# Weight pre-sums, product order and pair order in a one-core encoder layer

## The chip, the core and the metric

The kernel runs on one core of a Trainium2 chip. Its engines work in parallel, each through an instruction queue of its own, in order: TensorE (PE, matmul, with its weight loads shown as PEld), VectorE (DVE), ScalarE (ACT), GpSimd (POOL) and SyncE (SP), which issues most DMAs. The metric is device time of one execution in microseconds (us); lower is better.

## The reference

One layer of a streaming encoder over 1024 prompt rows and 32 sample rows of width 1024, in float32. Cut to what matters here:

```
h = rms_norm(x, g_mix)
q, k, v, ch, cb, cc, ga, gb = split(h @ w_in)          # one input projection, 6656 columns
a  = window_attention(q, k, v) @ w_attn_out
u  = cc * ch
bo = (cb * causal_conv3(u)) @ w_conv_out
x  = x + (sigmoid(ga) * a + sigmoid(gb) * bo) @ w_mix_out
x  = x + cross_attention(rms_norm(x) @ w_cq, mem_k, mem_v) @ w_co
x  = x + square(relu(rms_norm(x) @ w_up)) @ w_down     # 1024 -> 4096 -> 1024
y  = rms_norm(x, g_final)
```

The outputs also hold the last K/V rows, the convolution state and the memory K/V.

## The kernel before

**Layout.** Activations are kept transposed, features on the 128 partitions and rows along the free axis, in three chunks of rows: chunk 0 and 1 of 384, chunk 2 of 288 (`CH`, L23). Every float32 operand is split in a rounded high part and the rest (`split`, L119: a cast on ACT at L120, a subtraction on DVE at L121), and a product is three matmuls: high by high, high by low, low by high (`gemm`, L171 to L178). Weights come in tiles of 128x1024 on SP's queue (`fetch_w`), two ahead, and are split likewise.

**Stages.** (1) Start: load x, scale it by the norm's gain (L256, L257), sums of squares (`squares`, L301), first keys and values. (2) Attention: blocks of scores, softmax and values, interleaved with input projections. POOL scales the softmax rows there (L550). (3) The pairs. (4) The last gate columns and the attention output (`do_attn_out`, L982). (5) Conv-out, mix, cross-attention and the first up columns, chunk beside chunk. `do_conv_out` (L1036) multiplies its product by a gate (DVE, L1045), adds the attention part on POOL (L1048) and splits the sum for the mix product. (6) Pairs of up columns. (7) The down product.

**Pairs.** In stages 3 and 6 two weight tiles times chunks 0 and 1 are computed by a Strassen-like scheme with seven half-size products in place of eight. It needs combinations of activations (`x_kind`, L765, tiles tk and X) and of weights (`pair_issue`, L801: four additions on POOL, L807 to L810, give tiles s for the weights numbered 3 and 4; every one of the four weights is then split). `XP` (L835) lists the 13 pairs of stage 3: C, H and B of columns 4 to 7 (the convolution), then b (one gate) of 2 to 7, then a (the other gate) of 0 to 7. `x_pair` (L881) computes one pair and calls `after(name)` at named points (B11, W1, W4, W3, W2), where the next pair's loads and weights are issued. The first product of a pair (`x_p1`, L863) is copied by ACT to a tile s1 (L867) before the second (`x_p2`, L870) is accumulated on the same PSUM tile. Chunk 2 gets plain products (`x_c2`, L874, PSUM tile pa). `x_start` (L933) does these for the first two pairs ahead of the loop. A C column ends in a DVE and a POOL multiply (L596, L597), an H column in a DVE multiply (L601), a B column in three taps and two multiplies, a gate column in a DVE multiply and a sigmoid on ACT (L643, L644) with a store to sg_d.

**Weight sums.** The down product's scheme needs sums of four quarters of each of 32 pieces of `w_down`. `sum_step` (L705) issues from POOL a load of the next piece into SBUF (L710), then makes the four additions for the piece loaded one call earlier (L715) and issues from POOL its store to wsum_d (L716). Tiles alternate between `xacc` (one buffer, free during the whole first half) and `ws` (one buffer in the current stage's pool, L701 to L703). Calls are written at three slots of each of the four attention rounds (L730), and 22 times in stage 4 (L1001 to L1011).

**Order of the work.** The program text gives a priority, not the final order: a planner with a simulated timeline lays out each engine's queue ahead of time, may put a ready instruction ahead of one written before it, and the queues then run in that fixed order.

Of the kernel before, what the change touches and what calls it, by code (L numbers as in the profile page):

```python
# [18 lines left out]
P = 128  # L19
# [19 lines left out]
def hybrid_step(ctx: ExitStack, tc: tile.TileContext, io):  # L39
# [5 lines left out]
    def nm(s):  # L45
        uid[0] += 1
        return f"{s}_{uid[0]}"
# [221 lines left out]
    def norm_x():  # L269
# [31 lines left out]
        def squares(c):  # L301

            n = CH[c][1]
            sums = []
            for e, h in ((dve, 0), (pool_e, 4)):
                acc = st.tile([P, n], F32, tag=f"sum{h}", bufs=2 - h // 4, name=nm("sum"))
                for f in range(h, h + 4):
                    sq = acc if f == h else tmp(n)
                    if c == 0 and h:
                        pool_e.tensor_tensor(sq, raws[c][:, f], raws[c][:, f], op=ALU.mult)  # L310
                    else:
                        act.activation(sq, raws[c][:, f], AF.Square)
                    if f > h:
                        e.tensor_tensor(acc, acc, sq, op=ALU.add)
                sums.append(acc)
            accs[c] = sums
# [379 lines left out]
    W = {}  # L696
    pieces = [(j, t, i) for j in range(4) for t in range(2) for i in range(4)]

    def sum_tile(n):

        if n % 2:  # L701
            return xacc_tile()[:, :1024].rearrange("p (q c) -> p q c", q=4)
        return W["pool"].tile([P, 4, 256], F32, tag="ws", name=nm("ws"))  # L703

    def sum_step(load=True):  # L705
        old = W.pop("new", None)
        if load and pieces:
            at = pieces.pop(0)
            t = sum_tile(len(pieces))
            pool_e.dma_start(t, io["w_down"][at])  # L710
            W["new"] = at, t
        if old:
            at, t = old
            for to, x, y in ((3, 2, 3), (2, 0, 2), (0, 0, 3), (1, 1, 0)):
                pool_e.tensor_tensor(t[:, to], t[:, x], t[:, y], op=ALU.add)  # L715
            pool_e.dma_start(wsum_d[at], t)  # L716

    for kv, starts in enumerate([(0, 1, 3, 5, 6, 8, 10, 11, 13)] * 3 + [(0, 1, 3, 4, 6, 7, 8, 10, 11)]):
        base = 15 * kv
        units = [Unit(kv, p) for p in range(9)]  # L720
        for unit, k in zip(units, starts):
            at(base + k + 3, unit.values)
        for unit, k in zip(units, starts):
            at(base + k, unit.scores)
        for unit, k in zip(units, starts):
            at(base + k + 2, unit.turn)
        if kv < 3:
            at(base + 10, lambda kv=kv: do_KS(kv + 1))
            at(base + 14, lambda kv=kv: do_KS_rest(kv + 1))
        for k in (3, 8, 13):  # L730
            at(base + k, sum_step)
    at(59, lambda: sum_step(False))
    for i, h in enumerate(h for stage in hosts for h in stage):
        extras = [(c, e) for c in range(2) for e in events.get(3 * i + c + 1, [])]
        pre = events.get(3 * i, [])
# [96 lines left out]
        issue_w()  # L832


    XP = [((w, f), (w, f + 1)) for f in (4, 6) for w in "CHB"]  # L835
    XP += [(("b", f), ("b", f + 1)) for f in (2, 4, 6)] + [(("a", f), ("a", f + 1)) for f in (0, 2, 4, 6)]
    LATE = 3
    xs1, xemit = {}, {}

# [76 lines left out]
    def x_steps(i):  # L916
# [6 lines left out]
            todo["B11"] = lambda: x_fetch(i + 1)  # L923

        def after(what):
            todo.get(what, lambda: None)()
            if what == "B11" and XP[i][0][0] == "a" and "cv_cm" in S:
                closed(S.pop("cv_cm"))
                G["pool"] = ctx.enter_context(tc.tile_pool(name="gb", bufs=5, reuse_waits="tile", side="right"))
# [2 lines left out]

    def x_start():  # L933
        x_issue(0, 4)
        x_p2(0, x_p1(0))
        x_c2(0, 0)
        x_issue(0, 3)
        x_c2(0, 1)
        x_p2(1, x_p1(1))
        x_c2(1, 0)  # L940

    def s_begin():
# [59 lines left out]
    for f in range(4):  # L1002
        item(do_attn_out(f, range(3), [(0, sum_step)]), ("w_attn_out", f))
    for f in range(4, NF):
        item(do_attn_out(f, (0,), [(0, sum_step)]), ("w_attn_out", f))
    item(lambda: todo.extend((bcp, bc_d, 0, k) for k in range(NF)))
    for f in range(4, NF):
        item(do_attn_out(f, (2,), [(2, sum_step), (2, lambda: loads(2))]), ("w_attn_out", f))
    item(lambda: todo.extend((bcp, bc_d, 2, k) for k in range(NF)))
    for f in range(4, NF):  # L1010
        item(do_attn_out(f, (1,), [(1, sum_step), (1, lambda: loads(2))]), ("w_attn_out", f))  # L1011
    run()
    while pieces or "new" in W:
        sum_step()
    todo.extend((bcp, bc_d, 1, k) for k in range(NF))
    closed(W["cm"])
    closed(x_cm)
# [230 lines left out]
    def up_part(w, c, j):  # L1248
# [7 lines left out]
        else:  # L1256
            dve.tensor_scalar_max(t, a, 0.0)
        h = tmp(n)
        pool_e.tensor_tensor(h, t, t, op=ALU.mult)  # L1259
        hidden(c, j, h)  # L1260

    def do_up(j, c):
# [250 lines left out]

    def up_start():
        up_issue(0, 4)
        up_p2(0, up_p1(0))
        up_c2(0, 0, 1)
        up_issue(0, 3)
        up_c2(0, 1, 2)
        up_p2(1, up_p1(1))  # L1520
        up_c2(1, 0, 1)

    def up_steps(i):
# [20 lines left out]


    def up_last(i):
        up_p2(i, up_p1(i))
        wanted.extend([op_of("b11", k) for k in range(8)] + [h2_of(0, k) for k in range(8)])
        wanted.extend(op_of("b11", k) for k in range(8, 16))
        pump(4)  # L1550
        up_c2(i, 0, 1)
        pump(4)
        up_c2(i, 1, 2)
        pump(4)
        up_pair(i, up_steps(i), 2)
# [264 lines left out]
```

## Time and profile before

| | us |
|---|---|
| median of 3 runs | 1819.1 |
| the runs | 1818.11, 1819.1, 1920.33 |
| profiled execution | 1824.92 |
| its span, first to last instruction | 1823.0 |
| PE busy in the span | 1749.4 |
| DVE, ACT, POOL busy | 1205.6, 810.7, 755.4 |

Mean granted TensorE clock: 0.985 of full speed. A line of the timeline reads: start, duration, engine, line, operation, output<-inputs, shape, count, and in brackets how long the engine had been idle before it and what ended that. A line of a group reads: line, engine, operation, count | busy us in total, mean ns | idle before. A line of the waits reads: who waited for whom, total us, times, longest. Where the reading of one source line is shown, the durations are minimum/median/maximum in ns, then the first and last start.

### The profile page before, as it was taken

How to read it: one execution, taken by the hardware profiler on the slowest of the kernel's cores; microseconds unless marked ns; L12 is line 12 of the kernel's file. 1: busy time of each engine (PE TensorE's matmuls, PEld its weight loads, DVE VectorE, ACT ScalarE, POOL GpSimd, SP SyncE). 2: the span in 40 equal slices, each digit the busy share in tenths (PEclk: the TensorE clock that was granted, in tenths of full speed). 3: DMA queues.
4: the chain of work that ended last, by engine and by line, in shares of the span. 5: the costliest groups of instructions: out<-in, count | busy, mean ns of one | idle time of the engine just before them, and what ended most of it. 6: DMA issues, size and time to landing. Idle time of an engine off the chain costs nothing.

```text
span 1823.0 us, 30096 instructions
## 1 busy us (share of the span) xinstructions
PE 1749.4 (96%) x11016; PEld 1724.2 (95%) x11016; DVE 1205.6 (66%) x2080; ACT 810.7 (44%) x1561; POOL 755.4 (41%) x789
## 2 busy tenths in 40 slices
PE   6899999999899999997999989999999989999997
PEld 6899999999899999996999989999999989999997
DVE  7778786765867567455666777776656676436674
ACT  7546564554322335233465655642222343334453
POOL 4578868463654233323425152375654400100002
PEclk9999999999999999998999999999999999999998
DMA  6454433214122325688775767663343587446573
GB/s 223 155 186 147 153 129 104 74 55 139 65 70 78 111 85 178 217 282 283 275 244 198 244 209 249 237 211 133 138 138 125 162 291 231 154 133 204 191 252 104
DMA packets 177684, 312.50 MB, mean 171 GB/s; under 512 B 18016, under 2 KB 137600, under 8 KB 177408
## 3 DMA queue, kind: packets, MB, share of 16 engines
q1 hardware_dynamic: 168320, 277.02, 45.5%
q0 software_dynamic: 9216, 33.56, 5.2%
q8 instruction: 87, 1.43, 0.3%
q14 instruction: 61, 0.50, 0.1%
HBM read 232.70 MB, written 77.81 MB: 170 GB/s over the span
## 4 chain that ended last, share of the span: by engine, by line
PE 68%; DMA 15%; DVE 6%; POOL 5%; issue 4%; ACT 2%; SPq 1%; POOLq 0%; DVEq 0%; ACTq 0%
PE acc L176 7%; PE acc L177 7%; PE acc L178 7%; PE acc L825 6%; PE acc L826 6%; PE acc L827 6%; PE acc L1585 5%; PE acc L1586 5%; PE acc L1584 5%; DMA ws<-in_w_down 3%; DMA wsum_d<-ws 2%; POOL ws L715 2%; PE pa L177 2%; PE pa L176 2%; PE pa L178 2%
## 5 line engine op out<-in xcount | busy, mean ns | idle before, releaser
L121 DVE TENSOR_TENSOR wl<-wr,wh 128x1024 fp32r<-128x1024 f32 x222 | 301.5, 1358 | 110.5 <-ACT wh L120 106.4
L120 ACT CAST wh<-wr 128x1024 fp32r<-128x1024 f32 x222 | 233.0, 1049 | 313.1 <-PE acc L177 85.4
L176 PE MATMUL acc<-X,wh 128*128 128x384 f32 (+1 forms) x624 | 206.9, 332 | 12.9 <-ACT wh L120 9.9
L176 PE MATMUL acc<-Y,wh 128*128 128x384 f32 (+1 forms) x624 | 203.2, 326 | 13.0 <-ACT wh L120 12.7
L253 POOL TENSOR_TENSOR xacc<-xacc,ct 128x384 f32<-128x384 f32 (+1 forms) x62 | 77.2, 1247 | 319.2 <-ACT ct L251 317.0
L177 PE MATMUL acc<-X,wh 128*128 128x384 f32 (+1 forms) x624 | 205.0, 329 | 4.3 <-DVE X L257 4.3
L178 PE MATMUL acc<-X,wl 128*128 128x384 f32 (+1 forms) x624 | 204.6, 328 | 0.4 <-DVE wl L121 0.4
L178 PE MATMUL acc<-Y,wl 128*128 128x384 f32 (+1 forms) x624 | 202.4, 325 | 0.3 <-DVE wl L121 0.3
L177 PE MATMUL acc<-Y,wh 128*128 128x384 f32 (+1 forms) x624 | 202.3, 325 | 0.1
L550 POOL TENSOR_SCALAR S<-S,rec 128x256 f32<-128x256 f32 (+1 forms) x132 | 123.9, 951 | 25.6 <-DVE rec L548 25.4
L176 PEld LDWEIGHTS acc<-X,wh 128*128 128x128 f32 x624 | 119.6, 192 | 14.0 <-ACT wh L120 9.9
L176 PEld LDWEIGHTS acc<-Y,wh 128*128 128x128 f32 x624 | 117.7, 189 | 14.8 <-ACT wh L120 13.0
L177 PEld LDWEIGHTS acc<-X,wh 128*128 128x128 f32 x624 | 119.6, 192 | 6.0 <-DVE X L257 4.7
L178 PEld LDWEIGHTS acc<-X,wl 128*128 128x128 f32 x624 | 119.3, 191 | 1.8 <-DVE wl L121 0.9
L178 PEld LDWEIGHTS acc<-Y,wl 128*128 128x128 f32 x624 | 117.8, 189 | 0.8 <-DVE wl L121 0.8
L177 PEld LDWEIGHTS acc<-Y,wh 128*128 128x128 f32 x624 | 117.9, 189 | 0.3 <-DVE Y L121 0.3
L1584 PE MATMUL acc<-Y,wh 128*128 128x384 f32 (+1 forms) x352 | 113.2, 322 | 0.8 <-DVE lt L1362 0.7
L1585 PE MATMUL acc<-Y,wh 128*128 128x384 f32 (+1 forms) x352 | 113.2, 322 | 0.3 <-DVE Y L121 0.2
L1586 PE MATMUL acc<-Y,wl 128*128 128x384 f32 (+1 forms) x352 | 113.0, 321 | 0.0
L120 ACT CAST wh<-s 128x1024 fp32r<-128x1024 f32 x50 | 52.5, 1050 | 102.1 <-PE acc L826 57.3
L807 POOL TENSOR_TENSOR s<-wr 128x512 f32<-128x512 f32 x25 | 36.1, 1445 | 146.9 <-DVE wl L121 130.4
L1259 POOL TENSOR_TENSOR ct<-ct 128x288 f32<-128x288 f32 (+1 forms) x48 | 44.9, 936 | 117.4 <-DVE ct L1255 47.6
(359 smaller groups left out, 5312.7 us busy)
## 6 DMA issues: line engine op xcount, KB each, us to landing
wr<-in_w_in SPq DMA_DIRECT2D x56, 512.0 KB, 3.3
wr<-in_w_up SPq DMA_DIRECT2D x48, 512.0 KB, 3.8
wr<-in_w_down SPq DMA_DIRECT2D x32, 512.0 KB, 3.7
wr<-wsum_d SPq DMA_DIRECT2D x32, 512.0 KB, 3.6
wl<-wl_d SPq DMA_DIRECT2D x28, 512.0 KB, 4.6
wr<-in_w_conv_out SPq DMA_DIRECT2D x24, 512.0 KB, 4.8
wr<-in_w_mix SPq DMA_DIRECT2D x24, 512.0 KB, 4.6
ct<-b_d SPq DMA_DIRECT2D x48, 192.0 KB, 3.9
```

Of the source, the lines that this page charges most:

```text
L120: act.copy(hi, src)
L121: dve.tensor_sub(lo, src, hi.bitcast(F32))
L176: pe.matmul(out, wh[:, a], hi, start=(k == 0), stop=False)
L177: pe.matmul(out, wh[:, a], lo, start=False, stop=False)
L178: pe.matmul(out, wl[:, a], hi, start=False, stop=(k == len(acts) - 1))
L550: pool_e.tensor_scalar_mul(stl[:, h, :nk], stl[:, h, :nk], rec[:, h : h + 1])
L825: pe.matmul(acc, wh[:, a], hi, start=(start and k == 0), stop=False, skip_group_check=True)
L826: pe.matmul(acc, wh[:, a], lo, start=False, stop=False, skip_group_check=True)
L827: pe.matmul(acc, wl[:, a], hi, start=False, stop=(k == 3), skip_group_check=True)
L1584: pe.matmul(a, wh[:, s], hi, start=(start and k == 0), stop=False, skip_group_check=True)
L1585: pe.matmul(a, wh[:, s], lo, start=False, stop=False, skip_group_check=True)
L1586: pe.matmul(a, wl[:, s], hi, start=False, stop=(stop and k == len(acts) - 1), skip_group_check=True)
```

## The change

Five edits.

1. Sums of squares at the start: the four squares of chunk 0 that POOL made go to ACT.
2. Weight sums: two calls in each attention round in place of three (slots 5 and 12), 8 pieces; one piece in each of the 13 pairs, loaded into xacc after W3 and added and stored at the next pair's B11; the other 11 in stage 4, where the calls of the chunk-2 and chunk-1 columns are dropped.
3. Pair order: the gate pairs b(2,3) and b(4,5) come first, the rest follows as before.
4. `x_start`, `up_start` and `up_last`: the chunk-2 product of a pair is written between its first and second product.
5. Up stage: the square of the eight plain chunk-2 up columns goes from POOL to ACT.

```
@@ squares
-                    if c == 0 and h:
-                        pool_e.tensor_tensor(sq, raws[c][:, f], raws[c][:, f], op=ALU.mult)
-                    else:
-                        act.activation(sq, raws[c][:, f], AF.Square)
+                    act.activation(sq, raws[c][:, f], AF.Square)
@@ weight sums
-    def sum_tile(n):
-        if n % 2:
-            return xacc_tile()[:, :1024].rearrange("p (q c) -> p q c", q=4)
-        return W["pool"].tile([P, 4, 256], F32, tag="ws", name=nm("ws"))
-    def sum_step(load=True):
-        old = W.pop("new", None)
-        if load and pieces:
+    def sum_load(acc):
+        W["acc"] = acc
+        if pieces:
             at = pieces.pop(0)
-            t = sum_tile(len(pieces))
+            if acc:
+                t = xacc_tile()[:, :1024].rearrange("p (q c) -> p q c", q=4)
+            else:
+                t = W["pool"].tile([P, 4, 256], F32, tag="ws", name=nm("ws"))
             pool_e.dma_start(t, io["w_down"][at])
             W["new"] = at, t
+    def sum_add(old):
         if old:
             at, t = old
             for to, x, y in ((3, 2, 3), (2, 0, 2), (0, 0, 3), (1, 1, 0)):
                 pool_e.tensor_tensor(t[:, to], t[:, x], t[:, y], op=ALU.add)
             pool_e.dma_start(wsum_d[at], t)
+    def sum_step():
+        old = W.pop("new", None)
+        sum_load(not W.get("acc", True))
+        sum_add(old)
+    def sum_done():
+        sum_add(W.pop("new", None))
-        for k in (3, 8, 13):
+        for k in (5, 12):
             at(base + k, sum_step)
-    at(59, lambda: sum_step(False))
+    at(59, sum_done)
@@ order of the pairs
-    XP = [((w, f), (w, f + 1)) for f in (4, 6) for w in "CHB"]
-    XP += [(("b", f), ("b", f + 1)) for f in (2, 4, 6)] + [(("a", f), ("a", f + 1)) for f in (0, 2, 4, 6)]
+    XP = [(("b", f), ("b", f + 1)) for f in (2, 4)]
+    XP += [((w, f), (w, f + 1)) for f in (4, 6) for w in "CHB"]
+    XP += [(("b", 6), ("b", 7))] + [(("a", f), ("a", f + 1)) for f in (0, 2, 4, 6)]
@@ x_steps
         def after(what):
+            if what == "B11":
+                sum_done()
             todo.get(what, lambda: None)()
+            if what == "W3":
+                sum_load(True)
@@ x_start (up_start likewise; in up_last the pump calls stay around up_c2)
         x_issue(0, 4)
-        x_p2(0, x_p1(0))
+        A = x_p1(0)
         x_c2(0, 0)
+        x_p2(0, A)
         x_issue(0, 3)
+        A = x_p1(1)
         x_c2(0, 1)
-        x_p2(1, x_p1(1))
+        x_p2(1, A)
         x_c2(1, 0)
@@ attention output
-        item(do_attn_out(f, (0,), [(0, sum_step)]), ("w_attn_out", f))
+        item(do_attn_out(f, (0,), [(0, sum_step)] if pieces else []), ("w_attn_out", f))
...
-        item(do_attn_out(f, (2,), [(2, sum_step), (2, lambda: loads(2))]), ("w_attn_out", f))
+        item(do_attn_out(f, (2,), [(2, lambda: loads(2))]), ("w_attn_out", f))
...
-        item(do_attn_out(f, (1,), [(1, sum_step), (1, lambda: loads(2))]), ("w_attn_out", f))
+        item(do_attn_out(f, (1,), [(1, lambda: loads(2))]), ("w_attn_out", f))
     run()
-    while pieces or "new" in W:
-        sum_step()
+    assert not pieces and "new" not in W
@@ up_part
-        pool_e.tensor_tensor(h, t, t, op=ALU.mult)
+        if c == 2 and w[0] != "late":
+            act.activation(h, t, AF.Square)
+        else:
+            pool_e.tensor_tensor(h, t, t, op=ALU.mult)
```

More of the change, by code (lines that the diff above doesn't have):

```diff
@@ L1515, in up_start @@
         up_issue(0, 4)
-        up_p2(0, up_p1(0))
+        A = up_p1(0)
         up_c2(0, 0, 1)
+        up_p2(0, A)
         up_issue(0, 3)
+        A = up_p1(1)
         up_c2(0, 1, 2)
-        up_p2(1, up_p1(1))
+        up_p2(1, A)
         up_c2(1, 0, 1)
@@ L1546, in up_last @@
     def up_last(i):
-        up_p2(i, up_p1(i))
+        A = up_p1(i)
         wanted.extend([op_of("b11", k) for k in range(8)] + [h2_of(0, k) for k in range(8)])
@@ L1551, in up_last @@
         up_c2(i, 0, 1)
+        up_p2(i, A)
         pump(4)
```

## The prediction

> **What bounds the kernel now.** I read the page first, then the waits of PE, then stretches of the span, then single queues around the largest wait.
>
> ```profile
> PE 1749.4 (96%) x11016; PEld 1724.2 (95%) x11016; DVE 1205.6 (66%) x2080; ACT 810.7 (44%) x1561; POOL 755.4 (41%) x789
> ```
>
> The span is 1823.0 us, so PE is the bound and idles 73.6 us. The change alters no matmul, so it can win only idle time and time at a reduced clock. The waits of PE (total, times, longest):
>
> ```profile
> PE acc L176 <- ACT wh L120: 22.6, 2, 12.7
> ...
> PE acc L825 <- ACT s L867: 3.2, 2, 1.6
> ...
> PE acc L825 <- DVE u L601: 3.1, 1, 3.1
> ```
>
> The first holds the start of the kernel and one 12.7 us stop; the other two lie at the start of the pairs' stage. The stretches (length, busy PE, PEld, DVE, ACT, POOL, granted clock, DMA share, GB/s):
>
> ```profile
> 309.00:428.00 119.00, 119.00 (x780) 115.73 (x779) 82.43 (x224) 64.31 (x168) 57.49 (x82) 1.00 0.20 66
> 455.00:475.00 20.00, 15.26 (x73) 13.48 (x72) 15.88 (x20) 6.79 (x14) 13.52 (x13) 0.83 0.23 79
> 475.00:540.00 65.00, 64.28 (x398) 63.96 (x397) 51.52 (x64) 18.67 (x22) 40.63 (x36) 1.00 0.21 68
> 835.00:848.00 13.00, 0.38 (x3) 0.06 (x1) 0.80 (x1) 1.45 (x3) 5.94 (x8) 0.68 0.54 200
> 848.00:854.00 6.00, 5.69 (x19) 5.18 (x19) 5.96 (x9) 3.43 (x8) 1.25 (x1) 0.56 0.79 242
> ```
>
> PE stands still through 835 to 848 and then works six microseconds at a clock of 0.56. The pairs' stage after its start (475 to 540) is full. Why PE stops at 835, from the queues of POOL, DVE, ACT and PE:
>
> ```profile
> 701.98 0.63 POOL L710 DMA_DIRECT2D ws<-in_w_down  x1 [14.60 <-PE acc L827]
> ...
> 835.30 0.53 POOL L710 DMA_DIRECT2D ws<-in_w_down  x1 [6.76 <-DMA wsum_d<-ws]
> 841.39 3.12 POOL L715 TENSOR_TENSOR ws<-ws 128x256 f32<-128x256 f32 x4 [5.56 <-DMA ws<-in_w_down]
> ...
> 845.51 1.95 POOL L1048 TENSOR_TENSOR sgl<-sgl,ct 128x384 f32<-128x384 f32 x2
> 830.28 0.55 DVE L1045 TENSOR_TENSOR sgl<-acc,sgl 128x384 f32<-128x384 f32 x1
> 848.06 0.69 PE L176 MATMUL acc<-Y,wh 128*128 128x384 f32 x1 [12.68 <-ACT wh L120]
> ```
>
> The merge add L1048 had its input at 830.83 (830.28 + 0.55) but began at 845.51, because POOL's queue held the last weight sum ahead of it. ACT's split of the merge stood behind that add, the weight cast behind the split, PE behind the cast.
>
> **The sums.** Where do they run?
>
> ```profile
> L710 POOL DMA_DIRECT2D xacc<-in_w_down x16: 527/597/725, 1.3 to 296.2; - x16
> L710 POOL DMA_DIRECT2D ws<-in_w_down x16: 527/534/628, 102.4 to 835.3; - x16
> ...
> DMA to landing us min/median/max: 3.5/4.3/8.3
> ```
>
> ```profile
> L715 POOL TENSOR_TENSOR xacc<-xacc 128x256 f32<-128x256 f32 x64 | 54.9, 858 | 24.1 <-DMA xacc<-in_w_down 21.7
> L716 POOL DMA_DIRECT2D wsum_d<-xacc x16 | 9.6, 602 | 3.7 <-POOL xacc L715 3.5 <-POOL S L535 0.3
> ```
>
> This is the key reading. The program writes 12 sums into the attention stage and 20 into the attention-output stage, alternating between the tiles xacc and ws. Yet all 16 xacc sums were loaded between 1.3 and 296.2 us: the planner that orders each queue by a simulated timeline has drawn forward whatever needs no stage's memory. Only the ws sums keep their place, one tile, each load waiting for the store before it: from 701.98 to 845.5, which at the last load (835.30) is ten periods of 13.3 us, eleven sums.
>
> After the change the code alternates ws and xacc for 8 sums (4 each), takes xacc for the 13 pairs, and ws, xacc, ... ws for the last 11 (6 ws, 5 xacc): 22 xacc and 10 ws. **Late stop:** six ws sums from about 702 end near 702 + 6 x 13.3 = 782, far before 830. The 12.68 us go, and so does the slow clock behind them: 5.69 x (1 - 0.56) = 2.5 us. Upper bound 15.2. What is late next is the weight for conv-out: around 848 to 854 the DMA share is 0.79 and a cast waits on its load there, so I leave 1 us for it; lower bound 10, if half of the head start that the stop gave to the loads must be paid back. I take 14.
> The Trainium skill, "TensorE: Matmul & The Clock Gate", Part 1, has the half clock end after a sustained busy window of about 3.4 us; by that the clock term would be 1.7 us in place of 2.5, and the row decides.
>
> **Where the six more xacc sums go.** One costs POOL 4 x 0.858 for the adds, 0.597 to issue the load (median) and 0.602 the store: 4.6 us, six 28 us. Between 309 and 428 POOL is busy 57.5 of 119 us, the DMA share is 0.20 (each sum loads and stores a tile) and PE never idles, so I expect them there, before the pairs: 0 us. SP's queue isn't touched, since loads and stores of the sums are issued by POOL itself. Bounds: -1 (fewer sums in front of the softmax scaling) to +5 (one scaling held by a whole sum). If the planner keeps them in the pairs it is the third case below.
>
> **Chunk-2 product between the first two.** The order on PE and ACT at the start of the pairs:
>
> ```profile
> 441.96 0.29 PE L176 MATMUL pa<-X,wh 128*128 128x288 f32 x1
> 446.96 0.44 PE L825 MATMUL acc<-X,wh 128*128 128x384 f32 x1 [1.63 <-ACT s L867]
> 445.28 0.61 ACT L771 ACTIVATE lt<-lt,prm 128x384 f32<-128x384 f32 x1 [2.28 <-DMA lt<-in_x]
> 446.43 0.48 ACT L867 COPY s<-acc 128x384 f32<-128x384 f32 x1
> ```
>
> The chunk-2 product (pa) already runs at 441.96, before the second product at 446.96: the planner had made this swap. The second product still waits, because ACT copies s only after operand preparation (L771) whose DMA landed at 445.28. The swap alone therefore gives 0, here and in its two other places; between -0.5 and the 3.2 us of both waits.
>
> **Gate pairs first.** The first two pairs lose C's extra multiply:
>
> ```profile
> L597 POOL TENSOR_TENSOR Ga<-Ga,R 128x288 f32<-128x288 f32 (+1 forms) x3 | 4.2, 1410 | 0.0
> ```
>
> These 4.2 us stand on POOL between 445 and 465 among the operand preparation, which all of 455 to 475 waits for (4.7 us of idle and 20 x 0.17 = 3.4 us of clock). Three sigmoids come to ACT instead, which is busy 6.8 of 20. But the preparation also waits for its own loads, and a DVE read of a product bank (u L601, now a gate multiply) stays behind it in the queue. I take 2, between -3 (the sigmoids hold back a weight cast) and 8.1. The conv pairs move to a stretch that, at 475 to 540, shows no idle worth naming. On SP's queue the gates' stores to sg_d now go ahead of the convolution's stores to bc_d; both are read back only in later stages, so I cost that at nothing; without that distance a read would wait for one store to land.
>
> **Squares.** Eight chunk-2 squares leave POOL for ACT in the up stage, four leave POOL at the start:
>
> ```profile
> L1259 POOL TENSOR_TENSOR ct<-ct 128x288 f32<-128x288 f32 x8 | 8.8, 1105 | 8.8 <-issue 7.1 <-DVE ct L1255 1.8
> 1233.25 0.44 PE L825 MATMUL acc<-hx,wh 128*128 128x384 f32 x1 [1.78 <-ACT wh L120]
> 1167.61 0.43 ACT L251 ACTIVATE ct<-Ga 128x288 f32<-128x288 f32 x1
> L310 POOL TENSOR_TENSOR ct<-raw 128x384 f32<-128x384 f32 x3 | 2.4, 820 | 0.0
> 18.90 0.69 PE L177 MATMUL acc<-X,wh 128*128 128x384 f32 x1 [4.25 <-DVE X L257]
> ```
>
> Up stage: POOL wins 8.8 us ahead of the weight sums that the 1.78 us stop waited for; ACT gets at most 8 x 0.43 = 3.4 us, queued behind DVE's relu with weight casts behind them. I take 1.5, between -2 and 1.8. Start: 4 x 0.82 = 3.3 us leave POOL, four squares come to ACT (at the 0.43 us of the row above for fewer columns, about 2 us). The 4.25 us stop waits on DVE's X, which needs ACT's scaled copy first, so what DVE may win beside a quieter POOL the fuller ACT may cost: 0.5, between -2 (those squares ahead of the copies) and 4 (the stop gone).
>
> **Sum.** 14 + 0 + 0 + 2 + 1.5 + 0.5 = 18 us. The profiled execution took 1824.92 us, 1.9 more than its span; less 18 that is 1806.9. The median of the runs shown is 1819.1, 5.8 below the profiled one, so I predict 1801. The forecast's own range, from the bounds that are likely together, is 1793 to 1808.
>
> **Other ways.** *All start waits go too.* POOL freed at both starts lets the operands come in time: 15.2 late, 3.2 + 8.1 at the pairs (the second includes one wait of 1.6, so 9.7 together), 1.8 up, 3 start: about 30, time 1789. For it: POOL is busy 13.5 of 20 at 455. Against: the DMA that L771 waits for.
>
> *The late gain is given back.* Conv-out then starts without loads in hand and is limited by them: at 0.79 DMA share after 848 there is little to spare. Late gain 5, rest 0: 1814. Against: five fewer late ws sums lift as many loads and stores off the stage just before.
>
> *The sums really run in the pairs and hold POOL.* Then the sum's four adds and store stand in front of the four adds that make the fourth weight of the next pair. In the conv pairs:
>
> ```profile
> 487.60 1.61 POOL L809 TENSOR_TENSOR s<-wr,s 128x512 f32<-128x512 f32 x1
> 490.53 1.22 DVE L121 TENSOR_TENSOR wl<-s,wh 128x1024 fp32r<-128x1024 f32 x1
> 496.43 0.34 PE L825 MATMUL acc<-tk,wh 128*128 128x384 f32 x1
> L121 DVE TENSOR_TENSOR wl<-s,wh x50: 1209/1220/2041, 448.3 to 1439.2; 128x1024 fp32r<-128x1024 f32 x50
> ```
>
> That weight is ready at 491.75 and used at 496.43: slack 4.7. Against it stand 4.6 for the sum, up to 4.0 if its load lands at 8.3 instead of 4.3, and 2 x 0.82 for splits at their slowest: 10.2, so 5.5 late in each of six conv pairs, 33, less the 14 won: 19 slower, 1838. It decides from 7 us of delay a pair (4.7 + 14/6). At the median landing the delay is 6.2, and it ends 5 faster than before. Against it: the xacc rows above, which show such sums drawn forward.
> The Trainium skill, "SBUF — State Buffer", "SBUF: two separate sides", says GpSimd and a VectorE operation with two SBUF inputs share a port pair under an exclusive lock. By that the four adds would take up to 3.4 us from DVE in place of 1.6, and this case would end some 11 us later still; the slowest split, 2.04 against 1.22 us, points that way.
>
> **Chances.** Forecast 0.60; all waits go 0.14; gain given back 0.16; sums in the pairs 0.10 (under half of it slower than before). Eight in ten: 1786 to 1820. About 2% (36 us) is what a measurement can tell from no change; reaching 1782.7 needs half of all PE idle, 0.06; 1855.5 needs the third case with landing at its worst throughout, 0.04; within, 0.90.
>
> **What would show it.** Right: no stop of PE above 3 us between 820 and 850 of the old numbering; L1048 within 2 us of its DVE input; 22 xacc and 10 ws loads, the xacc ones done by about 430; the wait on s L867 still there. Wrong: a wait on wh L120 by a DMA in conv-out (given back); xacc loads between 470 and 700 with L825 waiting for wh (third case); or a new stop elsewhere from a queue that the planner ordered anew, which no row of before can show.

## The result, and the profile after

The changed kernel took 1806.85 us (median of 4 runs, 1805.75 to 1807.77) where the kernel before took 1818.61 (median of 4). The ratio is 0.9938, with a 95% interval of 0.9918 to 0.9957. On 1818.61 us that is a gain of 11.3 us, between 7.8 and 14.9, so less than the 2% that the prediction took as the least that can be told from no change, though the interval leaves 1 out. Two executions far above the rest, 1920.33 us of the kernel before and 2448.93 of the run with the up stage's squares on ACT, are in none of the ratios. Run again on another chip beside three other kernels it had a median of 1807.09 and a ratio of 0.9924 (0.9896 to 0.9953). The forecast was 1801, with 1793 to 1808 as its own range and 1786 to 1820 for eight in ten.

The profiled execution took 1805.75 us. The head of its page, with PE's busy time and share of the span:

```profile
span 1804.0 us, 30081 instructions
...
PE 1749.9 (97%) x11016; PEld 1725.4 (96%) x11016; DVE 1190.0 (66%) x2080; ACT 815.4 (45%) x1573; POOL 741.5 (41%) x777
```

PE's busy time is as before (1749.4) and its idle time has gone from 73.6 to 54.1 us. The waits of PE (total, times, longest):

```profile
PE acc L176 <- ACT wh L120: 8.3, 1, 8.3
PE acc L829 <- ACT tk L789: 6.6, 2, 4.1
PE acc L829 <- DVE lt L1365: 3.6, 1, 3.6
PE pt L555 <- POOL S L547: 3.3, 1, 3.3
```

The first wait is now the start of the kernel alone; the 12.7 us stop is gone. The waits on the copies s and on u at the start of the pairs are gone too, but a new one on operand preparation (tk) has come in their place, and it is as long. The stretches around the old stop, of the attention stage's last part and of the pairs (length, busy PE, PEld, DVE, ACT, POOL, granted clock, DMA share, GB/s):

```profile
820.00:850.00 30.00, 29.18 (x165) 28.36 (x164) 20.24 (x32) 15.52 (x26) 6.26 (x6) 1.00 0.99 349
...
309.00:428.00 119.00, 119.00 (x774) 115.96 (x774) 84.13 (x214) 63.30 (x162) 77.06 (x108) 1.00 0.33 109
455.00:475.00 20.00, 12.42 (x50) 11.47 (x51) 11.96 (x18) 7.54 (x14) 5.18 (x6) 0.83 0.25 84
475.00:540.00 65.00, 65.00 (x404) 65.00 (x403) 48.84 (x60) 21.22 (x28) 36.78 (x30) 1.00 0.23 78
```

Through 820 to 850 PE now works 29.18 of 30 us at full clock. From 309 to 428 POOL has taken up the added sums (77.06 us busy, 57.49 before) and PE still never idles. Where the sums run, from the loads (count, shortest/median/longest ns, first to last start) and from POOL's queue at the last sum and the first merge add:

```profile
L704 POOL DMA_DIRECT2D xacc<-in_w_down x22: 530/594/727, 1.3 to 383.2; - x22
L704 POOL DMA_DIRECT2D ws<-in_w_down x10: 530/540/623, 95.6 to 765.8; - x10
```

```profile
774.79 0.58 POOL L712 DMA_DIRECT2D wsum_d<-ws  x1 [0.41 <-POOL ws L711]
828.60 1.17 POOL L1058 TENSOR_TENSOR sgl<-sgl,ct 128x384 f32<-128x384 f32 x1 [53.23 <-DMA ct<-m_d]
826.32 0.55 DVE L1055 TENSOR_TENSOR sgl<-acc,sgl 128x384 f32<-128x384 f32 x1
```

So not one of the 13 sums that the program writes into the pairs runs there: all 22 xacc sums are loaded by 383, the last ws sum is stored at 774.79, and the merge add begins 1.7 us behind its DVE input (826.32 + 0.55 to 828.60).

At the start of the kernel the stop on DVE's X has shrunk from 4.25 us to 1.65 + 0.50:

```profile
14.97 0.44 PE L177 MATMUL acc<-X,wh 128*128 128x384 f32 x1 [1.65 <-DVE X L257]
16.26 0.69 PE L177 MATMUL acc<-X,wh 128*128 128x384 f32 x1 [0.50 <-DVE X L257]
```

### The profile page after: what moved, and what is told of

Read it like the earlier page. It is cut to its first block, busy times and chain, and to the rows that moved or that the text cites. A ratio compares the mean times of both kernels' runs of the same rounds, so it can differ in the third digit from the quotient of the medians.

```text
span 1804.0 us, 30081 instructions
## 1 busy us (share of the span) xinstructions
PE 1749.9 (97%) x11016; PEld 1725.4 (96%) x11016; DVE 1190.0 (66%) x2080; ACT 815.4 (45%) x1573; POOL 741.5 (41%) x777
## 5 line engine op out<-in xcount | busy, mean ns | idle before, releaser
L711 POOL TENSOR_TENSOR xacc<-xacc 128x256 f32<-128x256 f32 x88 | 76.8, 873 | 39.0 <-DMA xacc<-in_w_down 35.5
L121 DVE TENSOR_TENSOR Y<-ct,Y 128x384 fp32r<-128x384 f32 (+1 forms) x128 | 67.3, 556 | 34.6 <-ACT Y L120 34.3
```

What stands on the lines that cost most here:

```text
L121: dve.tensor_sub(lo, src, hi.bitcast(F32))
```

## The experiments

The twelve runs below fall into three series, each on one chip with the kernel before beside it. The kernel before had medians of 1828.44, 1821.12 and 1822.51 us there, and single runs from 1810.75 to 1832.28. That spread is a finding by itself, taken up below. Kernels are compared by their ratio to the kernel before of the same series; in the series this ratio is near the quotient of the medians, not equal to it.

### The kernel before, profiled again

> The kernel before, unchanged, profiled a second time. The first profiled execution took 1824.92 us where the runs of the same kernel have a median of 1818.61, and it stands 6.6 us behind the changed kernel already at the end of the start (a matmul of the first stage at 116.06 against 109.47). Theory: most of that lag is variation from one execution to the next, so this profile has a span of about 1817, its landmarks up to 116 lie some 5 us earlier, and the 12.7 us stop near 835 is there again with a length of 10 to 14. Rival: the lag at the start belongs to the kernel and the four squares gained it, then the span is again about 1823 and the start is as late as in the first profile.

Measured: span 1816.6. The same queues as in the prediction's largest fence, POOL and then PE:

```profile
828.82 0.53 POOL L710 DMA_DIRECT2D ws<-in_w_down  x1 [5.26 <-DMA wsum_d<-ws]
...
839.62 1.95 POOL L1048 TENSOR_TENSOR sgl<-sgl,ct 128x384 f32<-128x384 f32 x2
842.16 0.69 PE L176 MATMUL acc<-Y,wh 128*128 128x384 f32 x1 [5.42 <-ACT wh L120]
```

The stop is there with 5.42 us, not 12.68. The last ws load is issued at 828.82 where it was 835.30. The first late load was at 701.33 (701.98 in the first profile), so ten periods took 127.5 us here against 133.3. The stop is what is left of a chain of ten round trips after the time that other work covers, so 0.58 us in each trip make up 5.8 of the 7.3 us by which the two stops differ. The expected 10 to 14 us was wrong, while the span of about 1817 came out. Most of the lag at the start was not variation:

```profile
L558 PE MATMUL pt<-ident,S x248: 270/272/415, 114.3 to 420.6; 128*128 128x128 f32 x124
```

The first transposition of the attention stage is at 114.3. That is 1.8 us earlier than in the first profile and still 4.8 us behind the changed kernel's 109.5. So of the 6.6 us of lag the larger part belongs to the kernel, as the rival had it, though the rival's span of 1823 did not come again.

### The weight sums alone

```
+            if what == "B11":
+                sum_done()
...
+            if what == "W3":
+                sum_load(True)
...
-        item(do_attn_out(f, (2,), [(2, sum_step), (2, lambda: loads(2))]), ...)
+        item(do_attn_out(f, (2,), [(2, lambda: loads(2))]), ...)
```

> The kernel before with only the weight sums rearranged (8 in attention, 13 written into the pairs, 11 after), none of the other four edits. Theory: the late stop was the whole of the change's worth; no stop of PE over 3 us between 820 and 850, 22 loads into xacc of which none lies between 430 and 690, and the time is 10 to 15 us below the kernel before, about 1806. Rival, gain given back or spread over the edits: the time is 3 to 8 us below and the other four edits make up the rest of the 11.8 that the whole change measured.

Measured: 1816.23 us against 1828.44, ratio 0.9938 (0.9915 to 0.9961). No PE stop above 0.9 us between 820 and 870, and 22 xacc loads from 1.3 to 387.9. The theory holds for place and size, 11.3 us on that chip; the time of "about 1806" was wrong, as the whole level there was higher. That the late stop is the whole of the change's worth did not hold, as the start's squares show below.

### The kind of the tile alone

```
-        if n % 2:
+        if n % 2 or 12 <= n < 20:
             return xacc_tile()[:, :1024].rearrange("p (q c) -> p q c", q=4)
```

> The kernel before with one condition altered: eight of the sums that the program writes into the attention-output stage take the tile xacc in place of the tile ws (20 xacc and 12 ws in all, six ws late as in the changed kernel). No sum is written into the pairs. Theory: what counts is the kind of the tile, since the planner draws every xacc sum forward wherever it is written; then this kernel loses the late stop as the changed kernel does and takes 1804 to 1810 us. Rival, the place in the program counts: the xacc sums written late stay late, POOL's queue is as long as before at 830, the stop stays and the time is within 3 us of the kernel before, about 1818.

Measured: 1814.39 against 1828.44, ratio 0.9931 (0.9904 to 0.9958), the same as the rearranged sums within their intervals. The time lies above the expected 1804 to 1810, as the whole level of that chip did. PE has no stop above 0.83 us between 815 and 860. The loads:

```profile
L710 POOL DMA_DIRECT2D xacc<-in_w_down x20: 527/594/725, 1.3 to 360.3; - x20
L710 POOL DMA_DIRECT2D ws<-in_w_down x12: 527/540/623, 102.2 to 767.1; - x12
```

Eight sums written into the attention-output stage are loaded before 361 because their tile is an xacc. What the edit to the sums does is done by the kind of the tile; no part of the place in the program shows in the time.

### The sums held in the pairs

```
+            if after is not None:
+                pool_e.tensor_copy(t[:, 0, 0:2], after[:, 0:2])
             pool_e.dma_start(t, io["w_down"][at])
...
-                sum_load(True)
+                sum_load(True, raws["x", min(i + 1, len(XP) - 1)][3])
```

> The changed kernel with one small copy on POOL before each of the 13 pairs' loads: it takes two columns of the pair's fourth weight (s24) into the xacc tile, so that the load cannot be drawn forward out of its pair. The 13 sums really run in the pairs' stage. Third case of the prediction: a sum costs POOL 4.6 us a pair and waits for its load, the fourth weight (slack 4.7 us) comes late, PE waits up to 5.5 us in each of six conv pairs, and the time is 1822 to 1838, slower than the changed kernel by 15 to 33 us. Rival: the planner places load and adds behind the fourth weight's adds and the landing of 4.3 us is covered by the rest of the pair, then PE's waits in the pairs' stage stay under 3 us in all and the time is within 3 us of the changed kernel, about 1807.

Measured: 1808.49 against 1828.44, ratio 0.9895 (0.9866 to 0.9924). This is the lowest ratio of all; the changed kernel did not run on that chip, and its own intervals (0.9918 to 0.9957, 0.9896 to 0.9953) overlap this one, so which of the two is faster stays open. The pairs' stage after its start:

```profile
470.00:695.00 225.00, 225.00 (x1396) 225.00 (x1395) 160.66 (x201) 73.85 (x98) 160.54 (x162) 1.00 0.38 130
475.00:700.00 225.00, 224.86 (x1393) 224.39 (x1392) 153.00 (x200) 74.20 (x98) 102.31 (x85) 1.00 0.24 79
```

The first row is this run, the second the changed kernel over the same length of its pairs. POOL does 58 us more there, and PE does not idle at all. From 425 to 475, at the start of the pairs, PE waits 8.6 us here and 8.2 in the changed kernel. The third case of the prediction falls. The queue of POOL in this run shows why, with the split of the weight on DVE and its first use on PE as the last two rows:

```profile
555.17 1.29 POOL L815 TENSOR_TENSOR s<-wr,s 128x512 f32<-128x512 f32 x1
557.00 0.57 POOL L706 DMA_DIRECT2D xacc<-in_w_down  x1 [0.41 <-POOL xacc L705]
560.74 1.54 POOL L713 TENSOR_TENSOR xacc<-xacc 128x256 f32<-128x256 f32 x2 [3.17 <-DMA xacc<-in_w_down]
...
566.55 0.60 POOL L714 DMA_DIRECT2D wsum_d<-xacc  x1 [0.41 <-POOL xacc L713]
...
570.22 2.27 POOL L813 TENSOR_TENSOR s<-wr 128x512 f32<-128x512 f32 x1
562.29 2.04 DVE L121 TENSOR_TENSOR wl<-s,wh 128x1024 fp32r<-128x1024 f32 x1 [0.55 <-ACT wh L120]
570.57 0.33 PE L831 MATMUL acc<-tk,wh 128*128 128x384 f32 x1
```

The sum stands behind the adds that make one fourth weight (the last ends at 556.5), where the edit ties it, and its store is issued by 567.2, before the adds of the next begin at 570.22. The 13.8 us between the two hold the load's landing and the sum. The split of the first of these weights is stretched to 2.04 us and is still 6.2 us early (562.29 + 2.04 to 570.57).

### The other four edits, each alone

The start's squares on ACT:

```
-                    if c == 0 and h:
-                        pool_e.tensor_tensor(sq, raws[c][:, f], raws[c][:, f], op=ALU.mult)
-                    else:
-                        act.activation(sq, raws[c][:, f], AF.Square)
+                    act.activation(sq, raws[c][:, f], AF.Square)
```

> The kernel before with only the start's four chunk-0 squares moved from POOL to ACT. The prediction's term: 0.5 us gained, between 2 lost and 4 gained; time 1816 to 1820 at the median near 1818. Rival: the move is what takes the first wait of PE on DVE's X from 4.25 us to 1.65 us and the whole start ahead by up to 6 us; then the time is 4 to 6 us below the kernel before.

Gate pairs first:

```
-    XP = [((w, f), (w, f + 1)) for f in (4, 6) for w in "CHB"]
...
+    XP = [(("b", f), ("b", f + 1)) for f in (2, 4)]
+    XP += [((w, f), (w, f + 1)) for f in (4, 6) for w in "CHB"]
...
```

> The kernel before with only the order of the pairs altered (two gate pairs first). The prediction's term: 2 us gained, between 3 lost and 8.1 gained. Rival, from the changed kernel's trace: the operand preparation of the pairs is not brought forward by it (PE waits there 2.5 and 4.1 us on ACT's tk), and three sigmoids on ACT cost what three multiplies on POOL gave; then the time is the same within 2 us or up to 3 us longer.

The chunk-2 product between a pair's first two (one of three places):

```
-        x_p2(0, x_p1(0))
+        A = x_p1(0)
         x_c2(0, 0)
+        x_p2(0, A)
```

> The kernel before with only the three swaps in the program's text (chunk-2 product between a pair's first two). The prediction's term: 0, because the order on PE already had the chunk-2 product first, and the wait on the copy s stays. Rival: the copy s moves ahead of operand preparation in ACT's queue, the waits on s (3.2 us in two) go, and the time falls by up to 3 us, or the preparation behind the copy is that much later and nothing is won.

The up stage's chunk-2 squares on ACT:

```
+        if c == 2 and w[0] != "late":
+            act.activation(h, t, AF.Square)
+        else:
-        pool_e.tensor_tensor(h, t, t, op=ALU.mult)
+            pool_e.tensor_tensor(h, t, t, op=ALU.mult)
```

> The kernel before with only the chunk-2 squares of the up stage moved from POOL to ACT. The prediction's term: 1.5 us gained, between 2 lost and 1.8 gained; the 1.78 us stop near 1233 is the whole of what can be won there. Rival: that stop stays at its length (in the changed kernel it is still 1.28 us) and the time is the same within 1 us.

Measured, against 1821.12:

| edit alone | median us | ratio | 95% interval |
|---|---|---|---|
| squares of the start | 1815.65 | 0.9954 | 0.9929 to 0.9978 |
| gate pairs first | 1821.44 | 1.0008 | 0.9983 to 1.0032 |
| swap | 1818.03 | 0.9989 | 0.9967 to 1.0011 |
| squares of the up stage | 1818.57 | 0.9990 | 0.9966 to 1.0015 |

Only the start's squares move the time clear of the interval: 8.4 us by the ratio (4.0 to 12.9), 5.5 between the medians. DVE and POOL near 13 us, first in the kernel before and then in the changed one:

```profile
13.73 4.59 DVE L314 TENSOR_TENSOR sum<-sum,ct 128x384 f32<-128x384 f32 x1
...
13.77 0.84 POOL L310 TENSOR_TENSOR sum<-raw 128x384 f32<-128x384 f32 x1
14.56 2.38 POOL L310 TENSOR_TENSOR ct<-raw 128x384 f32<-128x384 f32 x3
16.91 0.98 POOL L314 TENSOR_TENSOR sum<-sum,ct 128x384 f32<-128x384 f32 x1
```

```profile
12.15 1.49 DVE L311 TENSOR_TENSOR sum<-sum,ct 128x384 f32<-128x384 f32 x1
13.57 2.63 DVE L257 SCALAR_TENSOR_TENSOR X<-raw,prm,X 128x384 fp32r<-128x384 f32 x2
...
12.20 3.59 POOL L311 TENSOR_TENSOR sum<-sum,ct 128x384 f32<-128x384 f32 x3
```

One VectorE add that at its median takes 0.56 us takes 4.59 while POOL runs four squares and an add without a gap, and the X that PE waits for is queued behind it. With the squares on ACT it takes 1.49. The Trainium skill, "SBUF — State Buffer", "SBUF: two separate sides", has GpSimd and a VectorE operation with two SBUF inputs share a port pair under an exclusive lock. The trace agrees that the VectorE operation is blocked; it was held through five POOL instructions and not one. By its record it began 0.04 us ahead of the first square (13.73 and 13.77), so having begun first did not get it through first.

The swap alone did move the second copy s (457.67) ahead of the casts of tk (461.59) in ACT's queue, where before the copy stood between them (458.87, 459.29). The wait on that copy went, but the one on the first copy was 2.73 us (1.63 before), and PE waited 2.77 us for a later weight's cast. The up squares left the stop on the weight at 0.97 us in the run alone and 1.28 in the changed kernel, from 1.78; at most a microsecond, which the interval can't tell from nothing.

In four of these profiles the eleven late sums are as in the kernel before. With its own two that makes six draws of the late stop:

| profile | stop on the weight near 835, us | first late load to last store, us | first late load to the merge add's input, us | span |
|---|---|---|---|---|
| before | 12.68 | 142.9 | 128.9 | 1823.0 |
| before, again | 5.42 | 137.7 | 129.0 | 1816.6 |
| squares of the up stage | 11.78 | 143.7 | 130.4 | 1829.5 |
| gate pairs first | 0.91 | 133.0 | 130.6 | 1812.1 |
| swap | under 0.5 | 129.1 | 129.5 | 1812.9 |
| squares of the start | under 0.5 | 131.7 | 130.2 | 1806.1 |

```profile
848.17 0.69 PE L176 MATMUL acc<-Y,wh 128*128 128x384 f32 x1 [11.78 <-ACT wh L120]
836.11 0.45 PE L176 MATMUL acc<-Y,wh 128*128 128x384 f32 x1 [0.91 <-ACT wh L120]
```

The first row is the up squares' run, the second that with gate pairs first. The six stops add up to 30.8, 5.1 each on average. The two middle columns show where they come from: the input of the merge add (the end of the first DVE multiply of conv-out) is ready 129 to 131 us after the first late load every time, while the chain of the sums takes anything from 129 to 144. The stop is long where the chain outlasts that time by much, and gone where it outlasts it by 1.5 us or not at all.

### Whether the changed kernel still varies

> The changed kernel itself, beside the three others of this series on one chip. In six profiles of kernels whose eleven late sums still run in ws the stop near 835 measured 12.7, 11.8, 5.4, 0.9, 0 and 0 us, and the kernel before varies from 1813 to 1832. Theory: the stop's length is chance of the transfers and the changed kernel has none, so its runs lie within 8 us of each other where those of the kernel before spread over 15, and its median is 11 to 18 us below. Rival: the spread comes from elsewhere (the start, the clock), then the changed kernel spreads as widely as the kernel before.

Measured: 1802.11 to 1810.83 in 8 runs, median 1807.09; the kernel before beside it 1810.75 to 1829.86, median 1822.51. The spread falls from 19 to 9 us (just above the expected 8) and what goes is the long end: the changed kernel's longest run equals the shortest of the kernel before. Eight runs spread less than 27 by their number alone, so the other kernels count too: in 11 or 12 runs each, the four with the late chain ahead of the merge adds spread over 20.6, 20.1, 17.0 and 11.7 us, and the two without it in 12 runs each (the merge adds on DVE, all sums in xacc, both below) over 8.6 and 6.4. The profile has no stop above 0.65 us between 820 and 855.

### Two edits in place of five

```
-        if n % 2:
+        if n % 2 or 12 <= n < 20:
...
+                    act.activation(sq, raws[c][:, f], AF.Square)
```

> The kernel before with two edits only: eight more sums in xacc tiles (as in the run that altered the tile's kind alone) and the start's four squares on ACT. Theory: these two terms are the whole change (late stop, and a VectorE add of the start that lasts 4.6 us beside POOL's squares and 1.5 without them); the time is within 2 us of the changed kernel run beside it. Rival: the pairs' order, the swaps and the up squares are worth the 2 and 1.5 us that the prediction gave two of them, or more; then this kernel is 3 to 6 us slower than the changed one.

Measured: 1807.81 us, ratio 0.9930 (0.9901 to 0.9960), beside the changed kernel's 1807.09 and 0.9924 (0.9896 to 0.9953). The theory holds within what the intervals show: two small edits give what the whole change gives. The intervals are some 5 us wide to each side, so a remainder of 2 or 3 us in the other edits is not excluded.

### The merge adds off POOL's queue

```
-            (dve if f == NF - 1 else pool_e).tensor_tensor(t, t, t1, op=ALU.add)
+            (dve if f == NF - 1 or (c == 0 and f < 3) else pool_e).tensor_tensor(t, t, t1, op=ALU.add)
```

> The kernel before with the merge adds of the first three conv-out columns of chunk 0 on DVE in place of POOL; all twenty late-written sums and their tiles stay as they were. Theory: the stop is nothing but these adds standing behind the last sum in POOL's queue, so without a single sum moved the stop near 835 is gone, and the time is that of the kernel with sums of another kind only, about 0.993 of the kernel before. Rival: conv-out waits there for its own loads, which the sums' transfers delay; then a stop of 3 us or more on a weight by a DMA takes its place and at most half of the gain is seen.

Measured: 1816.3 us, ratio 0.9977 (0.9956 to 0.9998). The queue of POOL still ends its last sum late, at 840.44 where the two profiles of the kernel before have 844.91 (a stop of 12.68 us) and 839.02 (5.42). The first merge add now runs on DVE at 830.14, and PE no longer stops:

```profile
840.44 0.58 POOL L716 DMA_DIRECT2D wsum_d<-ws  x1 [0.41 <-POOL ws L715]
842.20 0.99 POOL L1048 TENSOR_TENSOR sgl<-sgl,ct 128x384 f32<-128x384 f32 x1 [1.18 <-DVE sgl L1045]
...
830.14 0.56 DVE L1048 TENSOR_TENSOR sgl<-sgl,ct 128x384 f32<-128x384 f32 x1
...
839.76 0.45 PE L176 MATMUL acc<-Y,wh 128*128 128x384 f32 x1 [0.83 <-ACT wh L120]
842.22 1.04 ACT L120 CAST wh<-wr 128x1024 fp32r<-128x1024 f32 x1 [2.10 <-DMA wr<-in_w_conv_out]
```

So the stop is the merge add behind the last sum, as the prediction had it: it goes although no sum is moved and the chain takes 139.0 us, longer than in the second profile of the kernel before. The longest run is 1820.54, nine below the longest of the kernel before.

The ratio shows less than moving the sums did on the first chip (the intervals just overlap), and no more than the half that the rival allowed. The stop that the rival expected is not there: the longest wait on a weight is 0.83 us, and the casts that wait for their loads, as in the last row, do so in the changed kernel as well (0.85 to 2.18 us between 830 and 850). PE works 28.38 of the 30 us from 820 to 850, at a clock of 0.94 (29.18 at 1.00 in the changed kernel), so about 2.5 us are lost there against the changed kernel. The expected 0.993 also came from another chip. On this one the kernel with two edits has 0.9930; less the 5.4 us of the start's squares (taken up below) that leaves about 0.996 for the late stop, inside the interval here. How much of the difference is the chip and how much the loads stays open.

### All sums in xacc

```
-            if acc:
+            if True:
                 t = xacc_tile()[:, :1024].rearrange("p (q c) -> p q c", q=4)
```

> The changed kernel with every sum in an xacc tile, so that all 32 may be drawn forward and none waits for the store of the one before in a single ws tile. Theory: POOL has room before the pairs (57 of 119 us busy between 309 and 428 in the kernel before), the ten moved sums cost 10 x 4.6 = 46 us of it and hide; the time is within 2 us of the changed kernel, since its six late sums end 50 us before the first merge add. Rival: POOL is full by then, the softmax scalings and the operand preparation of the pairs stand behind sums, and the time is 3 to 10 us above the changed kernel.

Measured: 1810.15 us, ratio 0.9930 (0.9909 to 0.9951), no better than the changed kernel: 3.1 us above it between the medians, 1.1 by the ratios, with intervals that overlap. So it lies between theory and rival. The loads run from 1.3 to 538.4, so the sums did not all find room before the pairs; the last ones run in them. The attention stage starts at 110.5 (109.6 in the changed kernel beside it) and its last transposition is no later (417.0 and 418.2), but PE waits more in the pairs: 13.8 us from 425 to 560 in place of 8.5. The rows that are new or longer there (the second was 0.7):

```profile
PE acc L829 <- ACT s L872: 2.9, 2, 2.3
PE acc L829 <- DVE lt L902: 2.9, 2, 2.2
```

POOL makes adds of sums among the operand preparation at the start of the pairs (441.01, 443.91), which is the place that the rival named; that these adds cause the waits is not shown. PE also waits 6.1 us at the start of the down stage in this profile, on DVE's lt; whether that belongs to the edit is open. No kernel that ran beside the changed one beats it.

## Why the prediction was right and where its terms were wrong

**The reading of the planner was right.** 22 xacc and 10 ws loads, xacc loaded by 383 (forecast: by 430), the last late sum stored at 775 (forecast 782), no stop of PE, the merge add 1.7 us behind its input. The run that changes only the tile's kind shows that the kind is the cause of where they run, and the run with the merge adds on DVE that the stop is the merge add behind the last sum.

**The late stop: the mechanism was right, the size was one draw.** The term was 14, from a stop of 12.68 us and 2.5 us of slow clock. Over six profiles the stop averages 5.1. The clock term exists only behind the three long ones: PE's busy time times the missing clock in the six microseconds behind them is 2.5, 1.7 and 2.0 (in the second profile of before and in the up squares' run from these rows).

```profile
842.00:848.00 6.00, 5.58 (x22) 5.08 (x23) 5.86 (x9) 3.53 (x8) 1.25 (x1) 0.70 0.79 238
848.00:854.00 6.00, 5.58 (x21) 5.08 (x22) 5.85 (x9) 3.54 (x8) 1.25 (x1) 0.65 0.82 239
```

That is 6.2 over six, 1.0 each, so about 6 in all rather than 14. The estimate from the Trainium skill, "TensorE: Matmul & The Clock Gate", Part 1, was 1.7 for this clock term; the three measured ones begin at that value and go to 2.5. On the chip whose runs of the kernel before lay mostly at 1827 to 1831 the same edit gave 11.3 us. A stop that is there nearly every time would explain it; no profile shows that.

**The start's squares: the term was 0.5 with an upper bound of 4, and it measured about 5.** The eight profiles with these squares on POOL have the first transposition at 113.7 to 116.3, on average 115.1; the five with them on ACT and the sums free to be drawn forward have it at 109.3 to 110.5, on average 109.7 (with 13 sums held in the pairs it is 105.3). The gain lasts: the first late load, at 701.3 to 702.0 in the four profiles with the same order of pairs and sums, is at 696.6 with the start's squares alone moved. The prediction saw the 4.25 us wait on X and argued that ACT's fuller queue may cost what DVE wins. It took DVE's part for small because it did not open DVE's queue at that place: the 4.59 us add was there to be read. The bound was also too low. The wait on X is 2.1 shorter, and a later wait on an ACT copy fell too, from 3.02 us

```profile
62.75 0.69 PE L176 MATMUL acc<-X,wh 128*128 128x384 f32 x1 [3.02 <-ACT ct L444]
57.55 0.69 PE L176 MATMUL acc<-X,wh 128*128 128x384 f32 x1 [1.35 <-ACT ct L441]
```

(second profile of before, then after). In all eight profiles with the squares on POOL this wait is 2.8 to 3.0 us, in all six with them on ACT 1.3 to 1.4. The clock of the first 35 us is higher too in this pair of profiles:

```profile
0.00:35.00 35.00, 21.57 (x123) 20.62 (x124) 25.14 (x34) 22.98 (x46) 14.40 (x22) 0.90 0.75 275
0.00:35.00 35.00, 24.12 (x146) 22.86 (x147) 26.20 (x41) 28.80 (x62) 15.53 (x24) 0.95 0.78 287
```

PE is 2.55 us busier there, and 24.1 us at 0.95 in place of 0.90 are 1.2; with the 1.67 of the later wait that is 5.4. These two profiles are 4.8 apart, the averages 5.4. The clock part is the least certain: the granted clock of these 35 us is 0.90 to 1.00 with the squares on POOL and 0.95 to 1.00 with them on ACT.

**Gate pairs first: the term was 2 and is nothing** (1.0008, 0.9983 to 1.0032). The stage begins some 5 us earlier in the changed kernel; shifted by that, from 450 to 470, POOL is busy 9.86 us of 20 in place of 13.52 from 455 to 475. And yet PE's waits at the start of the pairs add up to 8.2 us (2.53, 0.89, 4.10, 0.65) where they were 7.1 (1.63, 1.61, 3.14, 0.72). At the head of the longest of these waits stands what the prediction named against the term, the operands' loads.

```profile
463.79 0.61 ACT L776 ACTIVATE lt<-lt,prm 128x384 f32<-128x384 f32 x1 [2.65 <-DMA lt<-in_x]
466.41 0.93 ACT L789 CAST tk<-lt 128x384 fp32r<-128x384 f32 x2 [2.00 <-DVE lt L781]
466.97 1.33 PE L829 MATMUL acc<-tk,wh 128*128 128x384 f32 x3 [4.10 <-ACT tk L789]
```

The scaling waits for its load, DVE's subtractions follow it, the cast follows those, and PE follows the cast. With the gate pairs first as the only edit the longest wait there is 3.71 us on DVE's gate multiply (465.50). It stands behind a subtraction of the preparation (465.02), which follows a scaling on ACT (464.38) that waited for its load: both things that the prediction had named against its 2 us. Its upper bound of 8.1 was also too high by 0.8, as it took the missing clock over all 20 us and not over the 15.26 that PE was busy. "The wait on s L867 still there" was wrong: the swap in the text did move that copy on ACT. Nothing was won by it that the interval shows: in the run with the swap alone another wait took its place.

**Six more xacc sums: 0, as forecast**, hidden between 309 and 428. **The swap: 0, as forecast**, with the reservation above. **The up squares: 1.5 forecast**, 0.5 us of the stop seen, and a ratio that holds both.

**The last step of the working was wrong in itself.** 18 was taken from the profiled 1824.92 us, which gave 1806.9, and then another 5.8 for the distance of that execution to the median. But that execution lay above the median largely because its stop was one of the long ones (the second profile, with a stop 7.3 us shorter, took 6.3 us less), and a stop that is removed can't also be kept as an offset. For that one execution the late term was about right: 12.7 + 2.5 for its own stop and 5.4 for the start make 20.6, and from the one profiled execution to the other the difference is 19.2 (1824.92 to 1805.75). Against the median the stop is worth less, and the terms are about 6 + 5.4 = 11.4, beside 11.8 between the medians (the interval of the gain is 7 us wide, so the closeness says little). Without the shift the forecast would have been 1806.9, with 1806.85 measured: partly by luck, since the start was priced at 0.5 and 3.5 were given to the gate pairs and the up squares.

**The rivals.** That all start waits go: the start's did, the pairs' did not. That the late gain is given back by conv-out's loads: not in the changed kernel (29.18 of 30 us busy at a DMA share of 0.99), and with the merge adds on DVE, where the sums still run beside conv-out, no wait on a weight is above 0.83 us. That sums in the pairs hold POOL: the sums did not run there, and where they were made to, PE lost nothing after the start of the pairs. That rival set landing, sum and slow splits against the slack of one weight, 4.7 us; in the run they fall into the 13.8 us that POOL has between the adds of two such weights. Its sentence drawn from the shared port fell with it: splits of 2.04 us do occur, and the slack takes them.

## What to carry to other kernels

A stop at the end of a chain of transfers is one draw of a wide distribution: profile the kernel a second time before pricing it, and don't subtract it from one execution and then shift by that execution's distance to the median. Where a planner orders the queues, ask which resource pins a piece of work, here the tile, before reading anything into its place in the program. A wait that holds PE is worth following into the queue of the engine it names: a group of instructions whose longest is eight times its median (558 and 4589 ns here) is worth opening at that instruction, even when the line's total is small.

## What the hardware did that was not expected

A VectorE add with two SBUF inputs was held 4.59 us by five POOL instructions that ran without a gap, the same within 0.01 us in all eight profiles with the squares on POOL (4.58 to 4.59). Beside three POOL adds, with no square among them, VectorE got through at 1.49 us for the add and 1.3 for each of its next two instructions. Why the squares shut it out and the adds did not is not settled by these runs. In the pairs, where POOL was made 58 us busier, the VectorE splits of the third and fourth weights only went from 1370 to 1421 ns on average, 1.3 us over 26 of them:

```profile
L121 DVE TENSOR_TENSOR wl<-s,wh 128x1024 fp32r<-128x1024 f32 x26 | 35.6, 1370 | 3.1 <-ACT wh L120 2.8
L121 DVE TENSOR_TENSOR wl<-s,wh 128x1024 fp32r<-128x1024 f32 x26 | 36.9, 1421 | 2.5 <-ACT wh L120 2.3
```

(the changed kernel, then the sums held in the pairs).
